# Weight parts begun one block ahead at a fixed place, and the mask and bias of attention laid elsewhere, in a hybrid attention block

## The chip, the cores and the metric

One core of a Trainium2 chip runs one layer of an encoder block on 1024 tokens of width 1024, all in float32. The metric is the device time of the whole program in microseconds (us); a lower time is better. TensorE (PE) multiplies matrices, its weight loads are PEld, VectorE is DVE, ScalarE is ACT, GpSimd is POOL, and SyncE (SP) issues transfers; ACT and POOL issue some too.

## The reference, cut to what matters

```python
n = rmsnorm(h, ln_g)
proj = n @ w_in                       # 1024 x 3104, split by columns:
qa, ka, va, qg, kg, vg, rg, zf, zb = jnp.split(proj, offsets, axis=-1)
y_na  = neighbourhood_attention(qa, ka, va, rpb)   # 8 heads x 64, softmax over a window
        # of 8 x 16 grid places: scores + rpb bias, -inf outside the window
y_gla = bidirectional_gla(qg, kg, vg, rg, zf, zb, ...)  # 4 heads, chunks of 64 tokens,
        # decayed states by a scan over 16 chunks, both directions; rmsnorm; * silu(rg)
h = h + concat([y_na, y_gla]) @ w_out
h = h + square(relu(rmsnorm(h) @ w_ff1)) @ w_ff2        # d_ff = 4096
out = rmsnorm(h)
```

## The kernel before

Activations lie transposed, features on the 128 partitions and tokens along the row. A float32 product is made of three matmuls on parts: each operand is split into a high part (rounded to the matmul's type) and a low part (the rest), and high x high, high x low and low x high are added up. The normalised input is held as `nh` and `nl`.

The input projection goes by blocks of 128 columns (`proj`, "proj" in the rows): blocks 0 to 3 are GLA's q and k, 4 to 7 its values (heads 0 to 3), 8 to 11 its output gates, 12 to 15 attention's q for pairs of heads, 16 to 19 its k, 20 to 23 its v. A block needs its weights in parts `wh` and `wl`. `weights` loads them from HBM into `wf` (512 KB, on SP), then ScalarE writes `wl = -wf` (L170), GpSimd issues a transfer that fetches the block a second time and adds it onto `wl` in a way that leaves the low part (L171), and ScalarE casts `wh` (L173). All three come from a pool `stg` of staging tiles that are used in turn, so the next block's `wf` is loaded when an older one has been read. `weights` asks for a high priority, and the tile scheduler decides where on ScalarE the pair stands; TensorE's order alone is kept as the program writes it.

TensorE's order is written by hand. GLA's four heads run one after the other: the gates (`la`, ScalarE's lt and lm, two scans on DVE into `b`), keys and queries with decay (`kD`, `kI`, `qD`), transposes (`kt`), states of each chunk (`c`, copied from PSUM into `st` by ScalarE at L555 and L558), the scan over the chunks on DVE (L576 and L579), scores within a chunk (`a`, masked by DVE into `asb`), output (`o`), squares (`osq`), their sum (`ov`) and the norm (nt, nu, ny), whose product goes into `yg` (L605). Between these steps tables of numbers put in matmuls of the projection blocks, by a queue `fill` of generators; a block's evacuations (rm and rt for gates, vtmp and vtok for values, qt for attention's q and k with a cast on ScalarE, L403, and on GpSimd, L407) come with them.

Attention then goes through four pairs of heads, eight blocks of 128 queries each: scores `sc`, DVE's sum with the bias `bt` and row minimum into `xsc` (L767), the exponential on ScalarE (L769), normalisation on DVE, transposes `pt` with a cast on ScalarE (L797) and a difference on DVE (L798), the transposed values `nvt`, and the product `no`. The mask `msk` (256 KB) is loaded by GpSimd, the bias of a pair of heads `bt` (384 KB) by SP, and DVE adds them (L713) ahead of the first score. Both lie in a pool "na" that is opened where GLA's pools have just been closed, in the same memory. PSUM banks are shared by name (`bank("s", ...)`, two in turn), so that a matmul waits until the bank's last readers are done.

After attention follow the output product and the MLP, half of the time, which the change doesn't touch.

Of the kernel before, what the change touches and what calls it, by code (L numbers as in the profile page):

```python
# [10 lines left out]
F32 = mybir.dt.float32  # L11
F32R = mybir.dt.float32r
U32 = mybir.dt.uint32
AF = mybir.ActivationFunctionType
# [4 lines left out]
P = 128  # L19
# [5 lines left out]
NB = 8  # L25
# [19 lines left out]
)  # L45
FILL_ORDER = (('v', 0), ('r', 0), ('v', 1), ('q', 1), ('r', 1), ('v', 2), ('v', 3), ('r', 3), ('r', 2), ('n', 0), ('k', 0))
SOON = 200
SOON_W = 100
SOON_O = 100
# [14 lines left out]
def block_kernel(ctx, tc, xT, g_mix, w_in, w_z, rpb, na_mask, gu, gb, g_gla, sel_f, sel_b,  # L64
                 rst, w_out, g_ff, w1, w2, g_fin, out):
    nc = tc.nc
    V, S, DMA, G = nc.vector, nc.scalar, nc.sync, nc.gpsimd
# [14 lines left out]
    def bank(tag, name):  # L82
        return ps.tile([P, H], F32, tag=tag, name=name)
# [77 lines left out]
    def weights(block, eng=None):  # L161


        with tc.high_priority(offset=SOON_W):
            wf = stg.tile([P, D], F32, tag="wf", name="wf")
            DMA.dma_start(wf, block)
            if eng is not None:
                return split(wf, eng)
            wl = stg.tile([P, D], F32R, tag="wl", name="wl")
            S.activation(wl, wf, AF.Copy, scale=-1.0)  # L170
            G.dma_start(wl, block, accum_op=ALU.add)  # L171
            wh = stg.tile([P, D], F32R, tag="wh", name="wh")
            S.copy(wh, wf)  # L173
            return wh, wl

    def split(wf, eng=None, steps=1):
        wh = stg.tile([P, D], F32R, tag="wh", name="wh")
        wl = stg.tile([P, D], F32R, tag="wl", name="wl")
        for i in range(steps):
            c = slice(i * D // steps, (i + 1) * D // steps)  # L180
            S.copy(wh[:, c], wf[:, c])
            (eng or V).tensor_tensor(wl[:, c], wf[:, c], wh[:, c].bitcast(F32), op=ALU.subtract)
        return wh, wl
# [47 lines left out]
    def proj_part(d, w, c0, n):  # L231
        c = slice(c0, c0 + n)
        return product(d[:, c0 % H:c0 % H + n], w, lambda k: nh[:, k, c], lambda k: nl[:, k, c])

    def proj(blk, evac):

        w = weights(w_in[blk], G if blk == 4 else None)
        for hf in range(2):
            d = bank("mm", f"proj{blk}_{hf}")
            yield from proj_part(d, w, hf * H, H)  # L240
            evac(hf, d)
# [143 lines left out]
    def perm(t, hf):  # L385
        return t.rearrange("p (b r c) -> p b r c", b=NB, r=ROWS)[:, :, hf * 8:(hf + 1) * 8, :]

    def nat(d):
        return d.rearrange("p (r b c) -> p b r c", r=8, b=NB)

    def na_proj(p, nm, parts, tmp):
# [3 lines left out]
        def ev(hf, d):  # L395
            t = tmp()
            with tc.high_priority(offset=SOON):
                V.tensor_tensor(t, d, rms[:, hf * H:(hf + 1) * H], op=ALU.mult)
# [32 lines left out]
    with pool("gla", R) as gp:  # L431
# [4 lines left out]
        def gla_v(h):  # L436
# [3 lines left out]
            def ev(hf, d):  # L440
                tmp = gp.tile([P, H], F32, tag="g1", name="vtmp", bufs=2)
                with tc.high_priority(offset=SOON):
                    V.tensor_tensor(tmp, d, rms[:, hf * H:(hf + 1) * H], op=ALU.mult)
# [9 lines left out]
        def gla_r(h):  # L453

            def ev(hf, d):
                c = slice(hf * H, (hf + 1) * H)
                t = gp.tile([P, H], F32, tag="g0", name="rt", bufs=2)
                m = gp.tile([P, H], F32, tag="g1", name="rm", bufs=2)
                with tc.high_priority(offset=SOON):
                    V.tensor_tensor(m, d, rms[:, c], op=ALU.mult)  # L460
# [161 lines left out]

        for kind, i in FILL_ORDER:
            gen = {"v": gla_v, "r": gla_r, "q": gla_qk, "n": first_q, "k": first_k}[kind](i)
# [45 lines left out]
    yhl, vhl = {}, {}  # L670
# [27 lines left out]
            V.tensor_tensor(hT[:, d, c], hT[:, d, c], o, op=ALU.add)  # L698

    with pool("na", L) as ap, pool("qkv", L) as qp:  # L700
        msk = ap.tile([P, 4, P], F32, tag="msk", name="msk")
        G.dma_start(msk, na_mask)

        def bias_for(p):


            bt = ap.tile([P, 2, 7, P], F32, tag="bt", name=f"bt{p}")
            DMA.dma_start(bt[:, :, 0:3, :], rpb2[:, 2 * p:2 * p + 2, :, :])
            rows = msk[:, 3:4, :].to_broadcast([P, 2, P])
            for i in range(2):  # L710
                for o, src, m in ((3, 1, rows), (5, 0, rows), (0, 0, msk[:, 0:3, :])):
                    n = 3 if o == 0 else 2
                    V.scalar_tensor_tensor(bt[:, i, o:o + n, :], bt[:, i, src:src + n, :], 8.0, m,  # L713
                                           op0=ALU.mult, op1=ALU.add)
            return bt

        def qk_tiles(p):

            f = lambda pl, tag: pl.tile([P, T], F32R, tag=tag, name=f"{tag}p{p}")
            q = q0 if p == 0 else [f(yn_p, "yn3"), f(qp, "qc")] if p == 2 else [f(qp, "qa"), f(qp, "qb")]  # L720
            return q, k0 if p == 0 else [f(qp if p % 2 else gk, f"k{i}{p % 2}") for i in range(3)]

        def na_v(p):

            vT = []

            def transposes():
                vhl[p] = ap.tile([P, NB, 2, P], F32R, tag="vhl", name=f"vhl{p}")
                for g in range(2):
                    tb = bank("mm" if p + 1 == NH // 2 else "t", f"nvt{p}_{g}")  # L730
                    for i in range(4):
                        j = 4 * g + i
                        PE.transpose(tb[:, i * P:(i + 1) * P], vT[0][:, j * P:(j + 1) * P], ident)
                    src = tb.rearrange("p (a h d) -> p a h d", a=4, h=2)
                    hi = vhl[p][:, 4 * g:4 * g + 4, :, 0:64]
                    with tc.high_priority(offset=SOON_V):
                        S.copy(hi, src)
                        V.tensor_tensor(vhl[p][:, 4 * g:4 * g + 4, :, 64:128], src, hi.bitcast(F32),
                                        op=ALU.subtract)

            def ev(hf, d):

                if not hf:
                    vT.append((gk if p % 2 else qp).tile([P, T], F32, tag=f"k2{1 - p % 2}", name=f"vT{p}"))
                with tc.high_priority(offset=SOON):
                    V.tensor_tensor(perm(vT[0], hf), nat(d), nat(rms[:, hf * H:(hf + 1) * H]), op=ALU.mult)
                if hf:
                    fill.later(NA_LATE, transposes, ("v", p))
            return proj(20 + p, ev)
# [85 lines left out]
        bt = bias_for(0)  # L835
        fill.run(NA_PRE)
        xs = softmax(0, 0, *qk, bt)
        for p in range(NH // 2):
            if p > 1:
                yn.append(yn_p.tile([P, T], F32, tag=f"yn{p}", name=f"yn{p}"))  # L840
            if p + 1 < NH // 2:
                nxt = qk_tiles(p + 1)
                fill.add(na_proj(p + 1, "q", nxt[0], qt))
                fill.add(na_proj(p + 1, "k", nxt[1], qt), ("k", p + 1))
                fill.add(na_v(p + 1), ("v", p + 1))
            pt = [[ap.tile([P, 3, 3, P], F32R, tag=f"pt{i}{j}", name=f"pt{p}{i}{j}") for j in range(2)]
                  for i in range(2)]
            ob = {}
            for b in range(NB):
                fill.at(NA_FILL, p, b, 0)  # L850
                if b + 1 < NB:
                    xn = softmax(p, b + 1, *qk, bt)
                fill.at(NA_FILL, p, b, 1)
                turn(p, b, xs, pt)
                if b + 1 == NB and p + 1 < NH // 2:
                    fill.until(("k", p + 1))
                    qk, bt = nxt, bias_for(p + 1)
                    fill.run(NA_NEXT)
                    xn = softmax(p + 1, 0, *qk, bt)
                xs = xn  # L860
                fill.at(NA_FILL, p, b, 2)
                if b == 2:
                    fill.until(("v", p))
                    pv(p, 0, pt, ob)
                if b > 1:
                    pv(p, b - 1, pt, ob)
                if b == 2 and p + 1 == NH // 2:

                    k_stack.close()
                    n_stack.close()  # L870
                    hT = ctx.enter_context(pool("h", R)).tile([P, NK, T], F32, tag="hT", name="hT")
                    a1 = ctx.enter_context(pool("a1", R))
                    yhl[0] = half(a1, "y0")
                    DMA.dma_start(hT[:, :, 0:H], xT[:, :, 0:H])
                    to_parts(0, KO[:2], V)
                    for d in range(NK):
                        fill.add(sums(0, d, KO[:-1], G, ahead=KO[2:-1] if d == 0 else ()))
            pv(p, NB - 1, pt, ob)
# [39 lines left out]
    wf = stg.tile([P, D], F32, tag="wf", name="wf")  # L918
# [337 lines left out]
    with tc.high_priority(offset=150):  # L1256
        for n in range(2):
            p, i = f1.order[n]
# [131 lines left out]
    for c0, n in ((H, H), (0, Q), (Q, Q)):  # L1390
# [3 lines left out]
        for d in range(NK):  # L1394
            o = bank("o" if d % 2 else "t", f"f7_{d}_{c0}")[:, :n]
            for k in range(4):
                w = [w7[:, d // 4 * 4 + k, x, d % 4 * P:(d % 4 + 1) * P] for x in range(2)]
# [102 lines left out]
```

## Time and profile before

| | |
|---|---|
| time, median of 3 runs | 1216.72 us (1216.63 to 1218.94) |
| the profiled execution: time, span | 1218.11 us, 1216.1 us |
| mean granted TensorE clock | 0.980 |
| TensorE busy | 1164.6 us, 96% of the span |
| GLA with the projections, about | 45 to 278 us |
| attention, about | 278 to 460 us |

The span is that of the profiled execution, the slowest core's first to last instruction; its time has about 2.0 us around that. In the rows below, a timeline row is start, duration (us), engine, line, operation, output<-input, size and, in brackets, the idle time before it and what ended it. A row of the chain is start, duration, engine, tile, line. A row of the waits gives engine and line <- what it waited for: us in all, times, longest.

### The profile page before, as it was taken

What the parts mean: (1) busy time and instruction counts of PE and PEld (TensorE: products, weight loads), DVE (VectorE), ACT (ScalarE), POOL (GpSimd) and SP (SyncE); (2) the same over time, 40 slices, a digit from 0 to 9 for tenths busy, and PEclk for the clock granted to TensorE, in tenths of its full rate; (3) what the DMA queues carried; (4) which work ended last, traced back from release to release, by engine and by line L of the source; (5) the groups of instructions that cost most, each with busy time, mean ns of one, the idle gap of its engine ahead of it and who ended that gap; (6) DMA issues with size and microseconds to landing.
All of it is one profiled execution on the core that took longest, in us unless ns stands there. A gap on an engine that the chain in (4) does not pass through costs nothing.

```text
span 1216.1 us, 15445 instructions
## 1 busy us (share of the span) xinstructions
PE 1164.6 (96%) x5632; PEld 953.5 (78%) x5632; DVE 874.8 (72%) x1558; ACT 665.2 (55%) x1222; POOL 246.4 (20%) x199
## 2 busy tenths in 40 slices
PE   9998899887999999998999999999999999999995
PEld 8876688665878878876778888888888888888775
DVE  8785768746768696575876885876858768587467
ACT  6755565743656674444653644545445364453664
POOL 4200000100110213441103140321403214032004
PEclk9998899988999999999999999999999999999998
DMA  7342132222223324330120211112111111111203
GB/s 233 86 98 67 35 70 47 72 57 57 60 58 83 70 69 170 105 138 1 54 67 19 70 59 58 41 52 70 56 58 43 53 70 53 56 48 53 70 1 139
DMA packets 40283, 84.03 MB, mean 69 GB/s; under 512 B 9264, under 2 KB 20656, under 8 KB 40208
## 3 DMA queue, kind: packets, MB, share of 16 engines
q1 hardware_dynamic: 36608, 71.11, 17.8%
q0 software_dynamic: 3456, 11.94, 5.4%
q8 instruction: 44, 0.72, 0.2%
q14 instruction: 31, 0.25, 0.1%
q10 hardware_dynamic: 144, 0.00, 0.0%
HBM read 78.85 MB, written 5.96 MB: 70 GB/s over the span
## 4 chain that ended last, share of the span: by engine, by line
PE 76%; DVE 13%; ACT 6%; issue 2%; DMA 1%; SPq 0%; POOL 0%; DVEq 0%; ACTq 0%; POOLq 0%
PE f L111 24%; PE u L111 21%; PE proj L111 15%; PE op L111 5%; PE sc L111 2%; PE no L111 2%; DVE st L579 1%; PE pt L116 1%; PE o L111 1%; DVE pl L973 1%; DVE asb L571 1%; DVE nf L903 1%; PE sb L111 1%; PE ob L111 1%; DVE st L576 1%
## 5 line engine op out<-in xcount | busy, mean ns | idle before, releaser
L995 ACT CAST ph<-A 128x512 fp32r<-128x512 f32 x166 | 102.9, 621 | 146.4 <-PE f L111 73.6
L973 POOL TENSOR_TENSOR ul<-uB,uh 128x512 fp32r<-128x512 f32 x84 | 109.1, 1317 | 330.5 <-ACT uh L1008 213.4
L111 PE MATMUL proj<-nh,wh 128*128 128x512 f32 x352 | 153.8, 437 | 6.8 <-DVE qd L265 5.0
L111 PE MATMUL f<-uh,ph 128*128 128x512 f32 x400 | 155.9, 390 | 1.5 <-ACT u L1016 1.3
L111 PE MATMUL f<-ul,ph 128*128 128x512 f32 x400 | 155.8, 389 | 0.1
L111 PE MATMUL f<-uh,pl 128*128 128x512 f32 x400 | 155.7, 389 | 0.0
L973 DVE TENSOR_TENSOR pl<-A,ph 128x512 fp32r<-128x512 f32 x166 | 112.7, 688 | 52.6 <-ACT ph L995 52.6
L111 PE MATMUL proj<-nh,wl 128*128 128x512 f32 x352 | 140.9, 400 | 0.0
L111 PE MATMUL proj<-nl,wh 128*128 128x512 f32 x352 | 140.6, 400 | 0.0
L1155 DVE TENSOR_TENSOR hT<-hT,f 128x512 f32<-128x512 f32 x168 | 113.0, 686 | 19.8 <-PE f L111 19.6
L111 PE MATMUL u<-n,ph 128*128 128x512 f32 x288 | 89.2, 391 | 2.0 <-ACT ph L908 2.0
L111 PEld LDWEIGHTS f<-uh,ph 128*128 128x128 f32 x400 | 75.1, 188 | 17.8 <-ACT u L1016 1.8
L111 PEld LDWEIGHTS proj<-nh,wh 128*128 128x128 f32 x352 | 68.2, 194 | 26.5 <-issue 5.9
L111 PEld LDWEIGHTS f<-ul,ph 128*128 128x128 f32 x400 | 75.1, 188 | 16.1 <-DVE ul L973 0.4
L111 PEld LDWEIGHTS f<-uh,pl 128*128 128x128 f32 x400 | 75.1, 188 | 15.6
L111 PEld LDWEIGHTS proj<-nh,wl 128*128 128x128 f32 x352 | 67.9, 193 | 15.5
L1008 ACT CAST uh<-uB 128x512 fp32r<-128x512 f32 x84 | 51.9, 618 | 51.1 <-PE f L111 33.0
L111 PE MATMUL u<-T,ph 128*128 128x512 f32 x256 | 79.2, 391 | 0.1
L111 PEld LDWEIGHTS proj<-nl,wh 128*128 128x128 f32 x352 | 68.3, 194 | 12.5 <-issue 2.2
L111 PE MATMUL op<-y,wh 128*128 128x512 f32 x240 | 76.9, 401 | 0.4 <-DVE y L680 0.4
L171 POOL DMA_DIRECT2D wl<-in_w_in x21 | 18.7, 891 | 266.7 <-ACT wl L170 248.6
L111 PE MATMUL u<-nt,ph 128*128 128x512 f32 x224 | 69.0, 389 | 0.0
(300 smaller groups left out, 2525.0 us busy)
## 6 DMA issues: line engine op xcount, KB each, us to landing
A<-in_w SPq DMA_DIRECT2D x64, 512.0 KB
wf<-in_w_in SPq DMA_DIRECT2D x22, 512.0 KB
wl<-in_w_in POOLq DMA_DIRECT2D x21, 512.0 KB, 7.8
wf<-in_w_out SPq DMA_DIRECT2D x17, 512.0 KB
hT<-in_xT SPq DMA_DIRECT2D x2, 2048.0 KB
xs<-in_xT SPq DMA_DIRECT2D x6, 512.0 KB
out<-hT SPq DMA_DIRECT2D x4, 512.0 KB
out<-hT SPq DMA_DIRECT2D x8, 256.0 KB
```

The lines of the kernel that those rows point to most:

```text
L111: m = nc.tensor.matmul(*args, **kw)
L116: tc.keep_in_program_order(nc.tensor.transpose(*args, **kw))
L171: G.dma_start(wl, block, accum_op=ALU.add)
L571: V.copy_predicated(asb[hf], sel.bitcast(U32).to_broadcast([P, 4, P]), src.rearrange("p (a b) -> p a b", a=4))
L576: V.scalar_tensor_tensor(st[0:64, i + 1, :], st[0:64, i, :], dec[0:64, i:i + 1], st[0:64, i + 1, :], op0=ALU.mult, op1=ALU.add)
L579: V.scalar_tensor_tensor(st[64:128, j - 1, :], st[64:128, j, :], dec[64:128, j:j + 1], st[64:128, j - 1, :], op0=ALU.mult, op1=ALU.add)
L903: V.scalar_tensor_tensor(dst, hT[:, d, hf * H:(hf + 1) * H], gff[:, d:d + 1], r, op0=ALU.mult, op1=ALU.mult)
L973: return kp(eng.tensor_tensor(l, x, h.bitcast(F32), op=ALU.subtract))
L995: kp(S.copy(ph, x))
L1008: kp(S.copy(uh, x))
L1155: kp(V.tensor_tensor(hT[:, d, c], hT[:, d, c], o[:, s], op=ALU.add))
```

## The change

Two parts. First, `weights` is now called for the next block as soon as the current one begins (a list `BLOCKS` names the order), and ScalarE's two instructions, now always `wl` first, then `wh`, are kept in program order. Block 4 goes through the same function. Second, the tiles of the pool "na" are made in a fixed order, which gives them other addresses: `msk` and the first pair's bias `bt0` now lie where GLA's `qD` and `kI` were, whose last readers are matmuls inside GLA, and no longer where the norm's working tiles were.

```diff
+BLOCKS = (4, 8, 5, 1, 3, 9, 6, 7, 11, 10, 12, 16, 20, 13, 17, 21, 14, 18, 22, 15, 19, 23)
...
             wl = stg.tile([P, D], F32R, tag="wl", name="wl")
-            S.activation(wl, wf, AF.Copy, scale=-1.0)
+            tc.keep_in_program_order(S.activation(wl, wf, AF.Copy, scale=-1.0))
             G.dma_start(wl, block, accum_op=ALU.add)
             wh = stg.tile([P, D], F32R, tag="wh", name="wh")
-            S.copy(wh, wf)
+            tc.keep_in_program_order(S.copy(wh, wf))
             return wh, wl
+
+    parts = {}
+
+    def block_parts(blk):
+
+        if not parts:
+            parts[blk] = weights(w_in[blk], G)
+        n = BLOCKS.index(blk) + 1
+        if n < len(BLOCKS):
+            parts[BLOCKS[n]] = weights(w_in[BLOCKS[n]])
+        return parts.pop(blk)
...
     def proj(blk, evac):
 
-        w = weights(w_in[blk], G if blk == 4 else None)
+        w = block_parts(blk)
...
     with pool("na", L) as ap, pool("qkv", L) as qp:
-        msk = ap.tile([P, 4, P], F32, tag="msk", name="msk")
+        ap.tile([P, 2, 3], F32, tag="sm", name="sm", bufs=4)
+        msk, bt0, pt0 = None, None, {}
+        for tag in ("pt00", "pt01", "x", "msk", "pt10", "pad", "bt", "pt11", "vhl"):
+            if tag == "msk":
+                msk = ap.tile([P, 4, P], F32, tag="msk", name="msk")
...
+            elif tag == "bt":
+                bt0 = ap.tile([P, 2, 7, P], F32, tag="bt", name="bt0")
...
         G.dma_start(msk, na_mask)
...
-            bt = ap.tile([P, 2, 7, P], F32, tag="bt", name=f"bt{p}")
+            bt = bt0 if p == 0 else ap.tile([P, 2, 7, P], F32, tag="bt", name=f"bt{p}")
```

TensorE's order is the same instruction for instruction, and each engine has as many instructions as before. In attention's first block the pools' other tiles (`pt`, `vhl`, `xsc`) are taken from the same list. Lines of the kernel after are 2 higher at the start of the file and 13 to 30 higher further on. What moves on ScalarE and GpSimd, at three places:

ScalarE in the first head, where GLA's gate (rt) meets the copies of the chunk states (`c` into `st`); wl and wh are those of block 1. Before:

```order
L173 CAST wh<-wf 128x1024
L465 ACTIVATE rt<-rt 128x512
L461 ACTIVATE rt<-rm 128x512
L170 ACTIVATE wl<-wf 128x1024
L462 ACTIVATE rt<-rt 128x512
L535 COPY kt_814<-kt_0_815 128x512
L463 ACTIVATE rt<-rt 128x512
L535 COPY kt_814<-kt_1_821 128x512
L465 ACTIVATE rt<-rt 128x512
L555 COPY st_827<-c_0_0_848 64x4x128
L558 COPY st_827<-c_0_0_848 64x3x128
L555 COPY st_827<-c_0_1_849 64x4x128
```

and after the change:

```order
L474 ACTIVATE rt<-rm 128x512
L478 ACTIVATE rt<-rt 128x512
L475 ACTIVATE rt<-rt 128x512
L548 COPY kt_821<-kt_0_822 128x512
L476 ACTIVATE rt<-rt 128x512
L548 COPY kt_821<-kt_1_828 128x512
L478 ACTIVATE rt<-rt 128x512
L172 ACTIVATE wl<-wf 128x1024
L175 CAST wh<-wf 128x1024
L568 COPY st_834<-c_0_0_855 64x4x128
L571 COPY st_834<-c_0_0_855 64x3x128
L568 COPY st_834<-c_0_1_856 64x4x128
```

The pair has gone from among the rt steps, where it stood apart and wh first, to right ahead of the first copy into `st`.

At the end of GLA's last head, ScalarE before (osq are the squares of the head's two halves, k00p and k10p the casts of attention's first keys, wh and wl those of block 13):

```order
L595 ACTIVATE osq<-o_0_2177 128x512
L173 CAST wh<-wf 128x1024
L170 ACTIVATE wl<-wf 128x1024
L403 CAST k00p_2118<-qt 64x8x64
L405 CAST k00p_2118<-qt 64x8x64
L403 CAST k10p_2119<-qt 64x8x64
L405 CAST k10p_2119<-qt 64x8x64
L595 ACTIVATE osq<-o_1_2200 128x512
```

and after the change, further on, at the end of the norm of that head's second half (xsc is attention's first exponential):

```order
L226 ACTIVATE nu<-ov_1_2268,small 128x512
L220 ACTIVATE ny<-nt,small 128x512
L227 ACTIVATE nt<-ny 128x512
L172 ACTIVATE wl<-wf 128x1024
L175 CAST wh<-wf 128x1024
L799 ACTIVATE xsc,sm<-xsc,sm 128x256 x2
```

Between the two osq only the four casts are left, and the pair of block 13 now follows the norm's last step. GpSimd at the same place, with what each row waits for (the names are counters of engines or of GpSimd's transfers, DMASW); first before:

```order
L407 TENSOR_TENSOR q_593<-qt,q_593 64x8x64 [waits Activation_49]
L407 TENSOR_TENSOR q_594<-qt,q_594 64x8x64 [waits Activation_49]
L171 DMA wl<-in_w_in 128x1024 [waits DMASW2_49,Activation_49]
L702 DMA msk<-in_na_mask 128x512 [waits PE_49,DVE_49,Activation_49,Pool_49]
L171 DMA wl<-in_w_in 128x1024 [waits DMASW3_49,Activation_49]
```

and after the change:

```order
L420 TENSOR_TENSOR q_594<-qt,q_594 64x8x64 [waits Activation_49]
L173 DMA wl<-in_w_in 128x1024 [waits DMASW1_49,Activation_49]
L173 DMA wl<-in_w_in 128x1024 [waits DMASW2_49,PE_49,Activation_49]
L731 DMA msk<-in_na_mask 128x512 [waits DVE_49,PE_49,Pool_49]
L173 DMA wl<-in_w_in 128x1024 [waits DMASW3_49,Activation_49]
```

msk's transfer no longer waits for ScalarE; the counts that it waits for on DVE and TensorE are unchanged, the product into `yg` of the last half (L605 before) and the last `ov`. Ahead of it stands now the transfer onto wl of block 13, right behind that of the block before.

In attention's first blocks of queries, ScalarE before (pt_1_0 and pt_1_1 are the second block's casts, wh and wl those of block 17, vhl casts the values):

```order
L797 CAST pt_2367<-pt_0_0_2406 128x2x128
L797 CAST pt_2369<-pt_0_1_2411 128x2x128
L173 CAST wh<-wf 128x1024
L170 ACTIVATE wl<-wf 128x1024
L769 ACTIVATE xsc,sm<-xsc,sm 128x384 x2
L797 CAST pt_2367<-pt_1_0_2457 128x3x128
L797 CAST pt_2369<-pt_1_1_2463 128x3x128
L737 CAST vhl_2475<-nvt_0_2476 128x8x64
```

and after the change:

```order
L827 CAST pt_2311<-pt_0_0_2417 128x2x128
L827 CAST pt_2315<-pt_0_1_2422 128x2x128
L799 ACTIVATE xsc,sm<-xsc,sm 128x384 x2
L172 ACTIVATE wl<-wf 128x1024
L175 CAST wh<-wf 128x1024
L827 CAST pt_2311<-pt_1_0_2468 128x3x128
L827 CAST pt_2315<-pt_1_1_2474 128x3x128
L767 CAST vhl_2319<-nvt_0_2486 128x8x64
```

The pair of block 17 has gone from ahead of the second pair of exponentials to behind it, right ahead of the casts. Other pairs have moved as well: that of block 9 (before at 103.9 us) behind three copies of `qd`, that of block 12 (before at 207.76 us) from ahead of GLA's kD exponential to behind the gate's last rt step, ahead of nu, and that of block 16 (before at 221.4 us) from behind the norm to ahead of the first q cast (L403), of which the second now comes after the first four copies into `st`. On SP, the load of wf for block 21 goes right ahead of that of bt0.

More of the change, by code (lines that the diff above doesn't have):

```diff
@@ L700, in block_kernel @@
     with pool("na", L) as ap, pool("qkv", L) as qp:
-        msk = ap.tile([P, 4, P], F32, tag="msk", name="msk")
+        ap.tile([P, 2, 3], F32, tag="sm", name="sm", bufs=4)
[3 more added lines that the diff above has]
+                msk = ap.tile([P, 4, P], F32, tag="msk", name="msk")
+            elif tag == "x":
+                ap.tile([P, 384], F32, tag="x", name="xsc", bufs=4)
+            elif tag == "pad":
+                ap.tile([P, 256], F32, tag="pad", name="pad")
+            elif tag == "bt":
+                bt0 = ap.tile([P, 2, 7, P], F32, tag="bt", name="bt0")
+            elif tag == "vhl":
+                vhl[0] = ap.tile([P, NB, 2, P], F32R, tag="vhl", name="vhl0")
+            else:
+                pt0[tag] = ap.tile([P, 3, 3, P], F32R, tag=tag, name=f"pt0{tag[2:]}")
         G.dma_start(msk, na_mask)
         def bias_for(p):
-            bt = ap.tile([P, 2, 7, P], F32, tag="bt", name=f"bt{p}")
+            bt = bt0 if p == 0 else ap.tile([P, 2, 7, P], F32, tag="bt", name=f"bt{p}")
             DMA.dma_start(bt[:, :, 0:3, :], rpb2[:, 2 * p:2 * p + 2, :, :])
@@ L727, in transposes @@
             def transposes():
-                vhl[p] = ap.tile([P, NB, 2, P], F32R, tag="vhl", name=f"vhl{p}")
+                if p:
+                    vhl[p] = ap.tile([P, NB, 2, P], F32R, tag="vhl", name=f"vhl{p}")
                 for g in range(2):
@@ L845, in block_kernel @@
                 fill.add(na_v(p + 1), ("v", p + 1))
-            pt = [[ap.tile([P, 3, 3, P], F32R, tag=f"pt{i}{j}", name=f"pt{p}{i}{j}") for j in range(2)]
+            pt = [[pt0.pop(f"pt{i}{j}") if p == 0 else
+                   ap.tile([P, 3, 3, P], F32R, tag=f"pt{i}{j}", name=f"pt{p}{i}{j}") for j in range(2)]
                   for i in range(2)]
```

## The prediction

> **What bounds the kernel now.** I read the page first: busy shares, the chain that ended last, the costliest groups.
>
> ```profile
> PE 1164.6 (96%) x5632; PEld 953.5 (78%) x5632; DVE 874.8 (72%) x1558; ACT 665.2 (55%) x1222; POOL 246.4 (20%) x199
> PE 76%; DVE 13%; ACT 6%; issue 2%; DMA 1%; SPq 0%; POOL 0%; DVEq 0%; ACTq 0%; POOLq 0%
> L111 PE MATMUL proj<-nh,wh 128*128 128x512 f32 x352 | 153.8, 437 | 6.8 <-DVE qd L265 5.0
> L171 POOL DMA_DIRECT2D wl<-in_w_in x21 | 18.7, 891 | 266.7 <-ACT wl L170 248.6
> ```
>
> TensorE is busy 96% and carries three quarters of the chain. The third row matters most for the first half of the change: the matmuls that read the weights (proj) idled 6.8 us in all, and 5.0 of it was ended by a DVE product, none by name by a weight transfer. Beginning weights earlier has nothing large to win. Next, busy time by stage (columns: us, PE, PEld, DVE, ACT, POOL busy, granted PE clock, DMA share, GB/s) and the list of waits:
>
> ```profile
> 100.00:150.00 50.00, 41.95 (x199) 32.20 (x198) 31.05 (x59) 29.51 (x46) 2.11 (x4) 0.83 0.22 53
> 150.00:200.00 50.00, 49.58 (x289) 40.44 (x289) 34.30 (x60) 29.64 (x48) 2.96 (x5) 0.99 0.29 64
> 250.00:300.00 50.00, 41.29 (x184) 31.63 (x183) 24.01 (x58) 22.16 (x43) 2.48 (x3) 0.83 0.22 55
> 300.00:450.00 150.00, 149.53 (x778) 120.64 (x778) 111.22 (x329) 97.64 (x238) 24.16 (x20) 1.00 0.27 62
> PE sc L111 <- DVE sm L767: 6.5, 1, 6.5
> ```
>
> Where GLA's heads hand over (100 to 150, 250 to 300; GLA ends at 278 us) TensorE has holes, and there a chain through ScalarE and DVE sets the time; from 150 to 200 and in attention (300 to 450) it has almost none, so a late evacuation is paid in full there. The largest hole, 6.5 us, is the one at the mask, msk.
>
> **The change part by part.** TensorE's order and the counts of instructions stay, so no work is added. The moved thing is the pair wl, wh, two ScalarE instructions of 1.05 us that follow each other 0.95 us apart (rows below), thus 2.0 us that stand before or behind others on ScalarE. After 450 us ScalarE's order is the old one: 0.
>
> *First head, 68 to 107 us.* ScalarE, then TensorE, then rows of the chain:
>
> ```profile
> 70.52 1.04 ACT L170 ACTIVATE wl<-wf 128x1024 fp32r<-128x1024 f32 x1
> 73.84 0.63 ACT L465 ACTIVATE rt<-rt 128x512 f32<-128x512 f32 x1 [0.28 <-DVE rt L464]
> 74.38 0.56 ACT L555 COPY st<-c 64x512 f32<-64x512 f32 x1
> 76.06 0.58 ACT L558 COPY st<-c 64x512 f32<-64x512 f32 x1
> 76.30 1.55 PE L111 MATMUL c<-vtok,kt 64*128 64x128 f32 x16
> 79.40 0.36 DVE st L576
> 106.08 0.70 DVE qd L265
> 106.92 2.90 PE proj L111 x6
> ```
>
> Before, wh and wl stood among the gate's rt steps, where ScalarE waits for DVE anyway. Now they stand behind the last rt and ahead of the four copies of c into st. The last rt comes only 0.4 earlier without them (it waits for DVE's rt, which waits for the rt before), so the first copy starts at 74.38 - 0.4 + 2.0 = 75.98, 1.6 later. The fourth copy, done at 76.64 before, frees the bank that the second half of c needs about 0.05 us later; so c, the remaining copies and the scan on DVE are 1.6 later, and from 79.40 to the last qd DVE works almost without a hole on the chain to proj at 106.92. **+1.6**. Ends: 0, if that DVE stretch has slack that I don't see, and +3.3, if the later start costs one more stretch at half clock (1.7, below). At 104 us wl, wh go behind three qd copies; DVE's products end that wait, so 0. The pair at 131 us stays. Between 153 and 172 TensorE has proj matmuls in hand and the evacuations behind the moved pairs have some 1.7 us until it takes their banks: 0; without that cover one pair would cost up to its 2.0.
>
> *Last two heads, 203 to 250 us.*
>
> ```profile
> 207.76 1.05 ACT L170 ACTIVATE wl<-wf 128x1024 fp32r<-128x1024 f32 x1
> 208.71 1.03 ACT L173 CAST wh<-wf 128x1024 fp32r<-128x1024 f32 x1
> 217.13 0.69 ACT L213 ACTIVATE nu<-ov,small 128x512 f32<-128x512 f32 x1 [0.30 <-DVE yg L467]
> 222.30 0.70 DVE rm L460
> 241.65 0.36 DVE st L579
> 242.03 1.31 DVE st L579
> 241.90 2.63 POOL L407 TENSOR_TENSOR q<-qt,q 64x512 fp32r<-64x512 f32 x2
> ```
>
> This pair leaves 207.76 and goes behind the second rt of L465, directly ahead of nu: that norm's chain (nu, DVE's nt, ny, yg, then rm at 222.30, which frees a bank for proj) becomes about 0.9 later. A next pair goes ahead of the copies into st, +0.4. And a second q cast now follows those copies, so POOL's L407 (1.3 us each) falls into DVE's scan; the last rows show a scan step at 1.31 instead of 0.36 us beside L407, which could add up to 1.0. I take **+1.3** (0.9 + 0.4, since most of L407 lay beside DVE work in the old order too), ends 0 and +2.4.
>
> *The mask, 260 to 290 us.*
>
> ```profile
> 261.42 1.05 ACT L173 CAST wh<-wf 128x1024 fp32r<-128x1024 f32 x1 [0.61 <-PE proj L111]
> 266.38 1.90 PE L111 MATMUL ov<-osq,ones 128*128 128x512 f32 x2 [2.13 <-ACT osq L595]
> 272.64 0.63 ACT L214 ACTIVATE nt<-ny 128x512 f32<-128x512 f32 x1
> 277.46 0.70 DVE yg L605
> 278.75 3.47 DMA msk<-in_na_mask
> 282.30 1.90 DVE bt L713 x5
> 284.59 0.69 PE L111 MATMUL sc<-k00p,q 128*128 128x384 f32 x1 [6.45 <-DVE sm L767]
> wl<-in_w_in POOLq DMA_DIRECT2D x2, 512.0 KB, 7.4
> msk<-in_na_mask POOLq DMA_DIRECT2D x1, 256.0 KB, 3.5
> 265.00:270.00 5.00, 3.62 (x7) 2.19 (x8) 1.73 (x3) 4.10 (x8) 0.00 (x0) 0.66 0.86 196
> 285.00:290.00 5.00, 4.87 (x14) 3.35 (x14) 4.19 (x17) 2.88 (x10) 0.00 (x0) 0.50 0.00 0
> ```
>
> The new places of msk and bt0 are memory that attention's early readers leave long before 278 us, but the listing of GpSimd's order shows msk's transfer still held by DVE and TensorE, and the counts it waits for are the old ones: yg's last product and the last ov. Only ScalarE's wait goes, and that one ended sooner (yg needs ScalarE's result). So the layout by itself moves nothing: 0. What does move here is a weights pair: it leaves the 2.0 us from 261.4 on, the k casts and osq come 0.9 earlier and the 2.13-us hole shrinks to about 1.2; all that follows, yg's end included, is 0.9 earlier. But the pair now stands after the last norm step (272.64 + 0.63 - 0.9 = 272.4), so its transfer is issued at about 273.5 on GpSimd, right ahead of msk, and frees wf for one more 512-KB load on SP right ahead of bt0. In the old trace that wl took 7.4 us from issue to landing beside such a load, with 0.86 of the DMA engines busy: until about 281. msk and bt0, together 640 KB, now run from 277.9 beside them instead of alone. At best msk lands 0.9 earlier (281.3), and 2.4 earlier if the smaller hole also spares the half clock behind it; at worst it starts when the weights are in, 281 + 2.9 (3.47 less GpSimd's 0.56 for the issue) = 283.9, or +1.7. I take **+0.5**, nearer the late end, because 1 MB is put on the engines in the 4 us before.
>
> On that order of transfers, the Trainium skill's page "DMA: Bandwidth & Descriptors" (section "Two DMAs through the same engine are not ordered") says that within a queue of one engine descriptors start in order. By it alone msk would take the late end, +1.7 instead of +0.5, and the sum would be 1.2 higher; the trace of before never shows the two back to back.
>
> *Attention's first head, 291 to 300 and 343 to 348 us.*
>
> ```profile
> 291.70 1.05 ACT L173 CAST wh<-wf 128x1024 fp32r<-128x1024 f32 x1 [2.16 <-PE proj L111]
> 293.13 0.55 DVE L767 CUSTOM_DVE_ANT_0 xsc<-sc,bt 128x384 f32<-128x384 f32 x1
> 293.62 0.60 ACT L769 ACTIVATE xsc<-xsc,sm 128x384 f32<-128x384 f32 x1
> 294.81 0.83 ACT L797 CAST pt<-pt 128x384 fp32r<-128x384 f32 x2
> 296.25 0.95 PE nvt L116 x8
> ```
>
> Before, ScalarE did wh, wl while it waited for DVE's first score (293.13), then both exponentials, then the pt casts at 294.81. Now the exponentials start at 293.15, the pair follows at 294.3, and the casts begin at 294.3 + 1.9 = 296.25: 1.44 later. DVE's pt follows them, and the nvt transposes at 296.25 take a bank that pt frees, with less than 0.1 us to spare. **+1.5**, and of the same kind **+0.4** near 345 us, where a pair goes ahead of a later pt cast. Ends 0 (if TensorE has one more bank than I think) and +2.6 (both in full). The pairs of the other attention blocks have more room.
>
> Sum: 1.6 + 1.3 + 0.5 + 1.5 + 0.4 = 5.3. The profiled execution took 1218.1, 1.4 over the median 1216.7; on the median that makes 1222.0.
>
> **The rivals.**
>
> *The mask is early after all.* If the old readers in the new place were all that msk waits for, it would land during GLA: the 6.45-us hole goes and with it most of the half clock from 285 to 290.5 (5.5 us at 0.50, 2.7 lost), -9.2, while the other terms stay (+4.8): 1216.7 - 4.4 = 1212.3. It decides as soon as msk and bt0 are issued before about 272 us. Against it stand the unchanged waits. 0.10.
>
> *Nothing measurable.* The delays of 1 to 1.6 us are each taken up by slack which one execution doesn't show, or given back at the msk landing, where everything meets again: 1215 to 1219. For it: the banks' margins of 0.05 us are modelled ends. Against it: DVE's stretch of 27 us without a hole. 0.22.
>
> *More half clock.* After a hole of 2.13 us the clock was 0.66 in the next 5 us, after 6.45 us 0.50; a stretch comes in about 3.4 us and costs 1.7. New holes of 1.5 us at 77 and 296 us and a longer one at 278 could bring two or three more: 5.3 + 3.4 to 5.1, 1225 to 1227. 0.12.
> The Trainium skill, "TensorE: Matmul & The Clock Gate" (Part 1, on the clock gate), states a free-running activity window of about 3.4 us after whose idling the clock is halved. The old trace agrees in length; whether a 1.5-us hole counts depends on where it falls in a window, and by the rule that is open.
>
> **How the numbers follow.** My forecast has 0.50 (1219.2 to 1226), with 0.06 left for a gain of other make: the smaller hole at 264 us at its best end (-2.4) with the delays at their lower ends. A measurement here can tell about 0.2%, 2.4 us, from no change. Slower by more: 0.50 + 0.12 = 0.62; within: 0.22; faster: 0.16. Range 1212.5 to 1227.5: from the early-mask case to the half-clock case; my own case alone is 1219 to 1226.
>
> **What would show it.** Right, if the profile after has the copies into st 1.6 later and the 5-us hole before proj at the same length but later; msk's issue still right after yg, landing at 282 to 285 plus the earlier shift; the pt casts behind wl near 295 in the old time and a new hole of about 1.5 us at nvt. Wrong, if msk is issued long before the last yg, if the hole before sc is under 3 us, or if c and nvt don't wait.

## The result

| | before | after |
|---|---|---|
| median of all runs | 1216.68 us (4 runs, 1214.42 to 1218.94) | 1224.28 us (4 runs, 1222.21 to 1225.14) |
| ratio | | 1.0060, 95% interval 1.0037 to 1.0083 |
| profiled execution: time, span | 1218.11, 1216.1 us | 1222.21, 1220.4 us |

The change costs 0.6%, some 7 us. The profiled execution of after is the shortest of its four, so its trace accounts for 4.3 us of span; what the others have more is taken up below (clock).

The page after, the same first rows as of before (busy, the chain by engine), then the windows and the waits of GLA and attention:

```profile
PE 1162.6 (95%) x5632; PEld 952.0 (78%) x5632; DVE 873.1 (72%) x1558; ACT 665.8 (55%) x1222; POOL 248.1 (20%) x199
PE 72%; DVE 15%; ACT 8%; issue 2%; DMA 1%; SPq 0%; POOL 0%; DVEq 0%; ACTq 0%
```

```profile
250.00:300.00 50.00, 38.41 (x184) 29.50 (x183) 24.17 (x57) 21.41 (x40) 2.28 (x3) 0.88 0.20 49
300.00:450.00 150.00, 148.15 (x771) 119.37 (x769) 109.38 (x327) 97.62 (x235) 23.77 (x20) 1.00 0.28 64
PE sc L113 <- DVE sm L797: 9.0, 1, 9.0
PE proj L113 <- DVE rm L473: 3.3, 1, 3.3
```

Work is unchanged; TensorE merely stands longer. Four points of the chain moved from TensorE to DVE and ScalarE. The hole ahead of sc grew from 6.45 to 9.0 us, and attention, which had almost no holes, now has some.

The timeline of ScalarE and TensorE in the first head, after:

```profile
73.38 0.63 ACT L478 ACTIVATE rt<-rt 128x512 f32<-128x512 f32 x1 [0.28 <-DVE rt L477]
73.92 1.04 ACT L172 ACTIVATE wl<-wf 128x1024 fp32r<-128x1024 f32 x1
74.87 1.04 ACT L175 CAST wh<-wf 128x1024 fp32r<-128x1024 f32 x1
75.81 0.57 ACT L568 COPY st<-c 64x512 f32<-64x512 f32 x1
78.13 1.16 PE L113 MATMUL c<-vtok,kt 64*128 64x128 f32 x14 [0.72 <-ACT st L571]
```

The last rt comes 0.46 us earlier than before (73.84), the pair stands behind it, and the first copy starts at 75.81 instead of 74.38: 1.43 us later. `c`, which ran through at 76.30, now waits twice for copies (0.35, then 0.72 us).

The mask: rows of the chain, of the transfers (the last number is us from issue to landing) and of TensorE, after:

```profile
274.92 0.70 DVE yg L618
275.73 6.46 DMA bt<-rpb
282.31 1.90 DVE bt L742 x5
msk<-in_na_mask POOLq DMA_DIRECT2D x1, 256.0 KB, 5.6
265.53 1.12 PE L113 MATMUL ov<-osq,ones 128*128 128x512 f32 x2 [1.26 <-ACT osq L608]
284.61 0.69 PE L113 MATMUL sc<-k00p,q 128*128 128x384 f32 x1 [9.00 <-DVE sm L797]
```

The hole at the last ov shrank from 2.13 to 1.26 us and yg ended 2.5 us earlier, at 275.6. msk and bt were issued right behind it, 2.6 us earlier than before, and the sums began at the same 282.3. bt's transfer took 6.46 us: it stood on SP behind the load of wf for block 21 (512 KB, issued 1.4 us ahead), while the transfer onto wl of block 13 (512 KB) ran on GpSimd's queue. What had moved by 279.5 us is shown further on, with the account of the prediction.

Attention's first head after, ScalarE and TensorE:

```profile
293.31 0.60 ACT L799 ACTIVATE xsc<-xsc,sm 128x384 f32<-128x384 f32 x1
293.91 1.04 ACT L172 ACTIVATE wl<-wf 128x1024 fp32r<-128x1024 f32 x1
295.80 0.84 ACT L827 CAST pt<-pt 128x384 fp32r<-128x384 f32 x2
296.91 1.12 PE L118 MATMUL nvt<-ident,vT 128*128 128x128 f32 x8 [1.21 <-DVE pt L828]
349.85 1.12 PE L118 MATMUL nvt<-ident,vT 128*128 128x128 f32 x8 [1.23 <-DVE pt L828]
```

Both pairs stand between the exponentials and the casts, and nvt waits 1.2 us behind each.

### The profile page after: what moved, and what is told of

Same layout as the page of the kernel before. It is cut to its first block, busy times and chain, and to the rows that moved or that the text cites. A ratio compares the mean times of both kernels' runs of the same rounds, so it can differ in the third digit from the quotient of the medians.

```text
span 1220.4 us, 15431 instructions
## 1 busy us (share of the span) xinstructions
PE 1162.6 (95%) x5632; PEld 952.0 (78%) x5632; DVE 873.1 (72%) x1558; ACT 665.8 (55%) x1222; POOL 248.1 (20%) x199
## 4 chain that ended last, share of the span: by engine, by line
PE 72%; DVE 15%; ACT 8%; issue 2%; DMA 1%; SPq 0%; POOL 0%; DVEq 0%; ACTq 0%
PE f L113 24%; PE u L113 21%; PE proj L113 12%; PE op L113 5%; PE sc L113 2%; PE no L113 2%; DVE st L592 1%; PE pt L118 1%; PE o L113 1%; DVE st L589 1%; DMA bt<-rpb 1%; DVE nf L934 1%; DVE pl L1004 1%; DVE asb L584 1%; PE ob L113 1%
## 5 line engine op out<-in xcount | busy, mean ns | idle before, releaser
L799 ACT ACTIVATE xsc<-xsc,sm 128x384 f32<-128x384 f32 (+1 forms) x64 | 37.3, 584 | 58.5 <-DVE sm L797 58.0
```

The source lines that it names most:

```text
L799: S.activation(x[:, :n], x[:, :n], AF.Exp, scale=-1.0, bias=sm[:, i, 0:1], accum_out=sm[:, i, 1:2])
```

## The experiments

Times are medians; each job ran the kernel before beside its kernels, and the ratio is to that. The orders of the engines are those of the kernel that each starts from, except where the text says what moves.

**One half of the change at a time.** `e1_weights` takes the hunks on `weights`, `block_parts` and `proj` alone, `e2_layout` those on pool "na" alone.

> The first part alone: weight parts begun one block ahead in a fixed order, the pool "na" as before. Theory (the moved pairs cost the time, the layout nothing): the whole of the loss, 1222 to 1224.5 us, with the same holes as the kernel after: c waits 0.5 to 0.8 us near 77, sc about 9 us before 284.6, nvt 1.2 us near 296 and 349. Rival (the new layout costs or gives something of its own): off from the kernel after by more than 2 us.

> The second part alone: the tiles of pool "na" in the new order, the weights as before. Theory: no change, 1216 to 1217.5 us, msk issued right after the last yg as before, hole before sc 6.4 us. Rival (msk waits only for the old readers of its own place): msk issued before 272 us, hole gone, 1207 to 1209 us.

| | us | ratio (95%) |
|---|---|---|
| e1_weights | 1222.88 | 1.0048 (1.0035 to 1.0061) |
| e2_layout | 1217.55 | 0.9995 (0.9983 to 1.0007) |

The weights carry the loss, the layout does nothing. TensorE, after ScalarE's and DVE's waits, in e1 (first row) and e2 (second):

```profile
78.17 1.16 PE L113 MATMUL c<-vtok,kt 64*128 64x128 f32 x14 [0.72 <-ACT st L571]
```

```profile
282.62 0.69 PE L111 MATMUL sc<-k00p,q 128*128 128x384 f32 x1 [6.47 <-DVE sm L784]
```

e1 has the new wait of c to the hundredth; e2 has the hole of before. In e2 msk even keeps its wait for ScalarE: that this one went in the kernel after is due to the pair ahead of msk on GpSimd, which waits for ScalarE already, and not to the layout (e1, which has the old layout, has lost that wait too).

**The layout made to work.** `e3_layout_tile` is e2 with

```diff
-    with pool("na", L) as ap, pool("qkv", L) as qp:
+    with tc.tile_pool(name="na", bufs=1, side=L, reuse_waits="tile") as ap, pool("qkv", L) as qp:
```

> As the layout alone, but the pool "na" is opened so that each tile waits for the last users of its own memory and not for all of the pools that lay there. Theory (waits of the whole pools were what held msk and bt): msk is issued right behind the weight transfer of block 13, near 264 us, bt near 264 to 265 us, both land by 272 us; the hole of 6.45 us before sc shrinks to under 1.5 us and most of the half clock after it goes: 1207 to 1210 us. Rival (something else late ends the hole, DVE's last yg or the sums bt): a hole of 2 to 4 us stays, 1211 to 1214 us.

1212.00 us, ratio 0.9946 (0.9933 to 0.9959). The issue of msk on GpSimd, then the chain, then TensorE:

```profile
262.22 0.86 POOL L718 DMA_DIRECT2D msk<-in_na_mask  x1
```

```profile
274.53 0.70 DVE ny L604
275.26 0.04 DVE yg L605
275.86 1.89 DVE bt L729 x5
278.15 0.44 PE L111 MATMUL sc<-k00p,q 128*128 128x384 f32 x1 [2.22 <-DVE sm L784]
```

msk leaves at 262.2 instead of 278.8 and the hole falls from 6.45 to 2.22 us: the waits for whole pools were what held the transfers. Whether waits by tile would do as much with the old addresses was not run. But the time and the rest of the hole are the rival's (1211 to 1214 us, 2 to 4 us): DVE makes the five sums only behind yg, and these 1.9 us are what is late next.

`e4_after_tile` makes the same edit in the kernel after:

> The kernel after, with tiles of the pool "na" waiting for the users of their own memory alone. Orders on all engines are those of the kernel after. Theory (the two halves of the change stand in each other's way: msk stands on GpSimd behind the transfer onto wl of block 13, bt on SP behind the load of wf of block 21, and both of these wait for the pair that now follows the last norm step): msk and bt are issued only about 1 us earlier, 274.5 to 275 us, bt lands about 281.5, hole 8 us, gain 0.5 to 1.5 us over the kernel after: 1221 to 1223.5 us. Rival (with the waits gone the layout works as in the kernel before, minus 6 us): 1216 to 1218 us.

1223.76 us, ratio 1.0056 (1.0041 to 1.0072): nothing won that can be told. Rows of the chain and of TensorE:

```profile
274.48 1.04 ACT wl L172
275.53 0.95 ACT wh L175
276.50 0.33 SPq L168
276.92 7.65 DMA bt<-rpb
286.96 0.69 PE L113 MATMUL sc<-k00p,q 128*128 128x384 f32 x1 [9.16 <-DVE sm L797]
```

bt has no wait left that counts, but stands on SP behind wf's load, that waits for wh, and wh has been moved behind the norm. The first half of the change shuts the door that the second one was meant to open. The mechanism is as expected; the gain of 0.5 to 1.5 us is not there, since bt took 7.65 us.

**Pairs put back.** In the kernel after, some blocks begin their weights in their own `proj` again, without the fixed order:

```diff
+LATE = (1, 12, 16, 17, 18)          # e5; (1,) e6; (17, 18) e7; (13,) e8
...
+        if blk in LATE:
+            parts[blk] = weights(w_in[blk], keep=False)
         n = BLOCKS.index(blk) + 1
-        if n < len(BLOCKS):
+        if n < len(BLOCKS) and BLOCKS[n] not in LATE:
```

> The kernel after, but the pairs of blocks 1, 12, 16, 17 and 18 are again begun by their own block, not kept in order: on ScalarE they stand where they stood before the change (blocks 1 and 17 wh first among the rt steps and ahead of the exponentials). Theory (these five pairs carry 1.6 + 1.3 + 1.9 us, measured in the trace as 1.45 + 1.2 + 2.4): about 5 us back, 1217 to 1219.5 us; no wait of c at 77 and none of nvt at 296 and 349. Rival (the loss is half clock that happened to fall otherwise): 1222 to 1225 us with those holes gone.

1217.94 us, ratio 0.9995 (0.9986 to 1.0004): all of the loss is recovered, as expected, with the hole of 9.1 us at the mask still there. These five pairs, with what moves beside them (some casts, and the pairs of blocks 21 and 22), are the cause; those of blocks 12 and 16 were not put back alone. The waits of TensorE in e5 between 40 and 450 us (the longest two, and those for the copies into st):

```profile
PE sc L114 <- DVE sm L801: 9.1, 1, 9.1
PE proj L114 <- DVE rm L477: 1.8, 1, 1.8
PE c L114 <- ACT st L575: 0.9, 2, 0.6
```

Of the wait of c at 77 us, which was to go, 0.34 us stays; nvt waits nowhere.

> The kernel after, but the pair of block 1 is again begun by its own block, among the rt steps of the first head. Theory (that pair alone held c and with it the chain to 107 us, +1.6): no wait of c over 0.4 us near 77, proj of block 3 begins near 107.0 as in the kernel before, 1.4 to 1.8 us faster than the kernel after: 1221 to 1223 us. Rival (the later start is given back at the next hand-over): no wait at 77, but within 0.7 us of the kernel after.

1224.07 us, ratio 1.0062 (1.0043 to 1.0082): no gain in the time. In the trace

```profile
77.38 1.15 PE L114 MATMUL c<-vtok,kt 64*128 64x128 f32 x14 [0.35 <-ACT st L575]
107.60 0.77 PE L114 MATMUL proj<-nh,wh 128*128 128x512 f32 x1 [4.99 <-DVE qd L282]
```

proj of block 3 begins at 107.60, against 108.34 after and 106.92 before: half of the 1.43 us. Most likely this is because wh and wl now stand together among the rt steps where they stood apart before: the last rt starts at 74.54, against 73.84 before. 0.7 us is less than these runs can tell; the expectation of 1.4 to 1.8 us is missed. The profiled execution shows how such a gain gets lost: one matmul starts 0.4 us ahead of after (218.27 against 218.66), and one a little later 2.2 us behind it (227.90 against 225.67), because the hole of 3.33 us at proj of block 12 is followed by half clock here and not in the profile of after. One row of windows of e6 (the third last column is the granted clock; after has 1.00):

```profile
225.00:230.00 5.00, 5.00 (x22) 4.04 (x21) 1.99 (x4) 2.96 (x7) 0.00 (x0) 0.71 0.00 0
```

> The kernel after, but the pairs of blocks 17 and 18 are again begun by their own blocks. Theory (these two made the holes of 1.2 us at nvt near 296 and 349, and in attention nothing gives time back): both holes gone, 2.2 to 2.8 us faster than the kernel after: 1220.5 to 1222.5 us. Rival (TensorE is ahead of its banks elsewhere and waits there instead): holes gone, no more than 1 us faster.

The pairs of blocks 21 and 22 move too in this run, each ahead of casts that they stood behind. 1222.66 us, ratio 1.0029 (1.0013 to 1.0046). The median lies above what the ratio says because 7 of the 12 runs took 1222.6 to 1223.4 us and the others 1216.1 to 1218.7. nvt near 296 runs without a wait,

```profile
299.82 1.12 PE L119 MATMUL nvt<-ident,vT 128*128 128x128 f32 x8
```

and so does the one near 349. By the median 1.6 us came back, by the ratio 3.8; the expected 2.4 lies between, and the times don't settle it closer. The trace does: ahead of the first nvt this execution is 4.3 us behind that of after (299.58 against 295.30, the same matmul; like e6 it had half clock at 220 to 230 us, granted 0.74 and 0.58), and at the second nvt 1.5 us (351.35 against 349.85). So 2.8 us came back at the two holes.

`e8_undo_mask_pair` puts back block 13, ahead of the mask. Not only that moves: the pair of block 17 goes back ahead of attention's second exponentials as well.

> The kernel after, but the pair of block 13 stands again between the two squares of GLA's last head; nothing else moves. Theory (the move gave 0.9 to 2.5 us ahead of the mask and the transfers in front of bt took them back): the hole at the last ov is 2.1 us again, bt lands about 3.5 us after its issue instead of 6.5, the hole before sc is 6.4 instead of 9 us, and the time is that of the kernel after within 1 us, 1222.5 to 1224.5 us. Rival A (the late transfers alone cost): 2 us faster than the kernel after. Rival B (the earlier k casts were worth something in the end): 2 us slower.

1223.50 us, ratio 1.0041 (1.0025 to 1.0058), within the expected range. That is in part luck: with block 17 the wait of nvt near 296 us is gone too, which by itself would give about 1.2 us. What the pair of block 13 is worth has to be read from the trace:

```profile
267.65 1.55 PE L114 MATMUL ov<-osq,ones 128*128 128x512 f32 x2 [2.17 <-ACT osq L612]
285.81 0.69 PE L114 MATMUL sc<-k00p,q 128*128 128x384 f32 x1 [6.46 <-DVE sm L801]
msk<-in_na_mask POOLq DMA_DIRECT2D x1, 256.0 KB, 3.5
```

The 2.17-us hole is back, msk takes 3.5 us instead of 5.6, and the hole at sc is 6.46: against after, the same matmuls start 1.21 us later ahead of this stretch (264.89 against 263.68, the first of the last head's ov) and 1.20 later at its end (285.81 against 284.61, sc). So what the moved pair won ahead of the mask, the half clock spared included, the transfers that it had put in front took back.

**The clock.** `e10_busy_hole` is the kernel before with matmuls whose result nobody reads, in the 5-us hole at 102 us:

```diff
+        if blk == 3:
+            idle = bank("t", "idle")
+            for _ in range(5):
+                PE.matmul(idle, ones, rms[:, 0:H], start=True, stop=True)
```

> The kernel before with five idle matmuls (128x512, 0.9 us each, their result is never read) in the 5-us hole of TensorE at 102 us, ahead of the first proj of block 3; nothing else moves. Theory (the half clock from 106 to 116 us follows from that hole and costs up to 5 us there): the clock stays full from 103 to 117 us and proj runs on at 106.9: 2.5 to 5 us less than the kernel before, since one to three stretches of 3.4 us at half clock go. Rival (the clock there has another cause, or the matmuls that follow wait for something else anyway): no change within 1 us.

1214.69 us, ratio 0.9971 (0.9960 to 0.9982). Windows of before, then of e10 (the third last column is the granted clock):

```profile
105.00:110.00 5.00, 3.08 (x9) 2.53 (x9) 2.35 (x3) 2.73 (x4) 0.85 (x1) 0.62 0.65 129
110.00:115.00 5.00, 5.00 (x18) 3.97 (x18) 0.00 (x0) 0.61 (x2) 0.40 (x2) 0.50 0.63 182
```

```profile
105.00:110.00 5.00, 4.30 (x24) 3.00 (x22) 2.54 (x4) 2.93 (x5) 0.85 (x1) 1.00 0.60 115
110.00:115.00 5.00, 5.00 (x22) 3.50 (x22) 0.97 (x2) 3.32 (x6) 0.40 (x2) 1.00 0.67 193
```

Full clock, although proj waits for the same qd. The half clock at 105 to 115 us came from that hole, and it cost some 3 us.

**A version that beats both.** `e9_sums_on_pool` is e3 with the first pair's sums of bias and mask on GpSimd:

```diff
+                if p == 0:
+                    G.tensor_scalar(bt[:, i, 0:3, :], bt[:, i, 0:3, :], 8.0, None, op0=ALU.mult)
+                    G.tensor_tensor(bt[:, i, 3:5, :], bt[:, i, 1:3, :], rows, op=ALU.add)
+                    G.tensor_tensor(bt[:, i, 5:7, :], bt[:, i, 0:2, :], rows, op=ALU.add)
+                    G.tensor_tensor(bt[:, i, 0:3, :], bt[:, i, 0:3, :], msk[:, 0:3, :], op=ALU.add)
+                    continue
```

> The layout with tile waits (on the weights of before), and the first pair's sums of bias and mask on GpSimd, a product by 8 and three sums for each head, in place of DVE, which did them only after the last yg. Theory (in the run of the layout with tile waits the hole of 2.2 us before sc was DVE's sums of 1.9 us behind yg): with sums that are done by about 276 us the hole falls to 0.5 to 1 us: 1 to 2 us less than the layout with tile waits, about 0.6 to 0.7% under the kernel before in the same runs. Rival (GpSimd's eight steps last beyond 277 us, since bt lands at about 272 us): no gain or up to 2 us lost against it.

1208.62 us, ratio 0.9926 (0.9915 to 0.9938). The median is 3.4 us under e3; the two ran in different jobs, and by the ratios the gain is 2.4 us, a little more than the expected 1 to 2. The hole at sc is 1.75 us and not 0.5 to 1, because DVE's norm steps ran longer beside GpSimd's steps (first row, the products; the sums follow until 275.7):

```profile
266.82 3.11 POOL L728 TENSOR_SCALAR bt<-bt 128x384 f32<-128x384 f32 x2 [4.00 <-DMA bt<-rpb]
273.69 1.12 DVE L216 SCALAR_TENSOR_TENSOR ny<-nt,ny 128x512 f32<-128x512 f32 x1
274.84 1.39 DVE L604 TENSOR_TENSOR ny<-yg,ny 128x512 f32<-128x512 f32 x1
```

They take 0.69 us in the kernel before.

`e11_best` adds idle matmuls as in e10 at six holes:

> The layout with tile waits and the sums on GpSimd, on the weights of before, and idle matmuls (128x512, their result never read) in six holes of TensorE: five at 102 us, one at the scores within a chunk of head 1, one ahead of proj of block 12, two at those of head 3, two at the last ov, one ahead of attention's second sc. Theory (a hole of 1.3 us and more can cost one stretch of 3.4 us at half clock, 1.7 us; that kernel's profile had about six such): at most two stretches stay, 4 to 8 us less: 1200.5 to 1204.5 us, about 1.1 to 1.4% under the kernel before. Rival (the idle matmuls push real ones back by as much as the clock gives): 1206 to 1209 us, as without them.

1201.64 us (1200.95 to 1203.00), ratio 0.9877 (0.9857 to 0.9896); the mean granted clock of the profiled execution is 0.994 against 0.980 before. 7 us less than e9 (6 by the ratios), within the expected 4 to 8. It keeps the weights of before; nothing of the first half of the change is in it.

## Why the prediction was right, step by step

The forecast was 1222.0 us, slower; measured are 1224.28. The terms, in us on the path, worked out from the starts of the same matmuls in both traces:

| step | predicted | measured |
|---|---|---|
| first head, copies into st | +1.6 | +1.43 at c, copies and c |
| last two heads | +1.3 | +1.5: holes 1.76 to 3.33 at proj of block 12 and 2.80 to 3.70 at a, less 0.6 at ov and 0.4 at c |
| mask | +0.5 | 0.0: -0.9 at ov, -1.7 of half clock spared behind it, +2.6 at sc |
| attention, 296 us | +1.5 | +1.2 |
| attention, 349 us | +0.4 | +1.2 |
| sum | 5.3 | 5.3 |

That the two sums agree to the tenth is luck: the errors of the terms (-0.2, +0.2, -0.5, -0.3, +0.8) happen to cancel, and the measured sum counts 1.7 us of spared half clock, which the forecast left out. In the measured times the change is 7.6 us (the medians), 2.3 more than forecast.

- That the layout moves nothing was right, and for the reason given, the unchanged waits (e2, e3).
- First head and last two heads: right in place and size in the trace, and in time shown by e5 together with attention. In time the first head alone is not shown: putting back its pair won nothing that can be told (e6). What of the 203-to-250 term is L407 beside the scan was not measured apart.
- Mask: the total is near the forecast, but that is luck. The late transfers cost 2.6 us, and 2.6 had been won ahead of them, 1.7 of it by spared half clock; without that I estimate +1.7 from the same figures (2.6 - 0.9), the late end that I had named and not taken. I let msk come last behind wl on its queue; msk landed at 281.8 and bt last, at 282.2, behind wf on SP, 6.46 us for 384 KB. Both waited for what stood ahead of them in their own queue. GpSimd's queue (q0) and SP's (q1) from 272 to 279.5 us (packets, MB, share of the engines' time):

```profile
q0 software_dynamic: 125, 0.51, 41.7%
q1 hardware_dynamic: 97, 0.40, 18.2%
```

That is less than the 512 KB (0.52 MB) of wl and of wf, so of msk and bt, issued at 276.20 and 275.73, nothing had moved by then. The Trainium skill's rule of starting order in a queue ("DMA: Bandwidth & Descriptors", section "Two DMAs through the same engine are not ordered") agrees with this.

- The mis-sized term is the second attention pair: +0.4 where 1.2 was measured. Its old rows show the same picture as the first (pair, exponentials, casts), and I should have priced both alike.
- Half clock was left out of the sum and stands as a rival. It is the likely source of what the measured times have over the forecast. Windows of e1, whose orders are those of the kernel after, and of after:

```profile
220.00:225.00 5.00, 2.10 (x5) 1.75 (x6) 3.50 (x6) 3.35 (x6) 0.00 (x0) 0.67 0.46 127
225.00:230.00 5.00, 5.00 (x20) 3.99 (x20) 2.42 (x4) 2.97 (x7) 0.00 (x0) 0.65 0.00 0
```

```profile
220.00:225.00 5.00, 2.39 (x11) 1.99 (x12) 3.77 (x6) 3.33 (x6) 0.00 (x0) 1.00 0.39 109
225.00:230.00 5.00, 5.00 (x37) 4.11 (x37) 3.86 (x7) 4.99 (x8) 0.54 (x1) 1.00 0.01 3
```

The same hole of 3.33 us ahead of proj of block 12 brings half clock in one execution and none in the other, and the profiled executions of the same order took 1226.0 (e1) and 1222.21 us (after). Of the six profiles with this hole, four have half clock behind it (e1, e4, e6, e7) and two have none (after, e8). Of the six where the hole is 1.8 us (before, e2, e3, e5, e9, e10), none has. So the moved pair of block 12 cost more in most profiles than its term says.

The profile of after accounts for its own 4.1 us. The terms make 5.3, and half clock spared between 106 and 120 us gives back 2.7; that leaves 2.6, and up to 560 us the trace shows just that (the same matmul starts at 559.01 before and 561.56 after). The other 1.6 come within the next few microseconds, in the MLP, which the change doesn't touch: one of its matmuls starts at 565.35 before and at 569.46 after. Windows there, before and after:

```profile
565.00:570.00 5.00, 5.00 (x22) 3.79 (x21) 1.45 (x3) 4.02 (x7) 0.00 (x0) 1.00 0.00 0
```

```profile
565.00:570.00 5.00, 5.00 (x13) 3.65 (x14) 1.15 (x2) 0.18 (x1) 0.00 (x0) 0.66 0.00 0
```

That the other runs of after are 1.4 to 2.9 us slower than the profiled one fits executions that got half clock at more places, as e1 did at block 12, but they have no trace, so that is argued and not shown.

## What to carry to other kernels

Where one engine is busy 96% and a second one frees its PSUM banks with hardly any time to spare, work moved to "earlier" on the feeder is only early if it stands where the feeder waits; between a matmul's result and its copy it costs most of its length (1.2 to 1.4 us of 2.0 here). A tile's address changes nothing while its pool waits for whole pools: look at the waits of the built program, not at the addresses. And before a transfer's wait is taken away, look at what stands ahead of it in its queue.

## What the runs showed that I had not expected

- Idle matmuls in six holes were worth more than either half of the change: 7 us (e9 to e11). A hole of 3.33 us was followed by half clock in four profiles of six, one of 1.8 us at the same place in none of six.
- Two transfers of 512 KB issued 1.4 to 2.1 us ahead of bt made its 384 KB take 6.46 us, and 7.65 us when issued 0.4 to 1.1 us ahead (e4); without them it took 4.0 us at most (e8, issued at 279.54, the sums that need it begun at 283.52).
- GpSimd's product of a 128x384 float32 tile by 8 took 1.55 us each (3.11 for two), its sum of two such tiles 1.0 to 1.35 us, and beside them DVE's two-input steps went from 0.69 to as much as 1.39 us.
